# First norm of a hybrid S5 and convolution block: statistics in four batches, rows from a broadcast column, large S5 arrays loaded behind the slabs

## Chip, cores and metric

The kernel runs on one core of a Trainium2 chip. The metric is the device time of one execution in microseconds (us): the median of several. A profiled execution, taken apart from these, gives the trace.

## What is computed

One layer of a trunk over 2048 latent tokens (1024 channels) with 256 context tokens ahead of them; everything is float32. What matters here is its first sub-layer:

```python
def rmsnorm(x, g):
    y = xf * lax.rsqrt(jnp.mean(xf * xf, axis=-1, keepdims=True) + EPS)
    return y * g
...
mod_l = silu(c) @ ada_w + ada_b          # six vectors of 1024: sh1, sc1, ...
nl = rmsnorm(h_lat, norm1_g) * (1 + sc1) + sh1     # 2048 tokens
nc = rmsnorm(h_ctx, norm1_g) * (1 + csc1) + csh1   # 256 tokens
zl = nl @ w_in                           # columns: S5 input 512 | conv 2*512 | gates 2*1024
zc = nc @ w_in[:, :512]
ys_l, _ = s5_mixer(zl[:, :512], zc[:, :512], ...)  # 32 groups, both directions
yb_l = conformer_branch(zl[:, 512:1536], ...)
h_lat = h_lat + g1 * gated_merge(zl, ya_l, yb_l, w_out)
```

The second sub-layer, a gated MLP, follows and is the same in both kernels.

## The kernel before

A float32 product is made as three TensorE products (lines L462, L463, L464) of operands that are split into a high and a low part: a weight chunk `w_ch` and a block's normed tokens, `nl0` to `nl3` for the four blocks of 512 latent tokens and `nlc` for the context; `h` and `l` at a name's end are the parts. ScalarE casts the high part, VectorE or GpSimd (L453) subtracts for the low one.

`phase1` goes as follows. `ada_first` takes eight slabs of 1 MB of `ada_w` from SyncE's DMA queue, multiplies each with the two conditioning vectors (L577, two records for a product), and turns the result into columns (16 small products, L586), from which the modulation's columns come. For the norm, x is needed in two layouts: `half_stats` loads 256 tokens with the token on the partition, squares them on ScalarE (L622) with the sum in a column, and takes the root (`rstd`: GpSimd's power, then a correction on VectorE). The tokens with channels on the partition come from `xt`. `row` turns two columns into a row that stands in all partitions: a diagonal tile `dg` for each column (L630), and a product with ones (L631). For the context and block 0, `early` multiplies xt by the row (L644), and `late` scales and splits (L650 to L654) once the modulation is there; for blocks 1 to 3, `modulate` does both in one pass (L661 to L663).

Then come the "u" GEMMs, that is the S5 input: for the context 96 products of 256 columns, for each of the blocks 96 of 512, in pairs of output tiles. `u_out` copies a result out of PSUM on ScalarE (L668) and stores it from ScalarE's DMA queue (`d_u`, L671). After them come the convolution's "v" GEMMs and the gates, of 24 products each: `v_pair` has four GEMMs whose sigmoid goes to `av` on ScalarE (L840) and four that multiply it on VectorE. With every GEMM goes S5 work in the background: 32 "tables" (`tab`, one for each group: three operations on GpSimd, three on VectorE, a copy and two sines on ScalarE, L245 to L253, then a store `d_rec`), 16 iterations of `s5_ops` (products L308, L318), and 32 groups of the scan. `caw` are rows of the convolution, multiplied at L795.

The order on each engine is set by a scheduler of the framework from the program and from `urgent` regions, and each engine and each DMA queue works strictly in its order. PSUM tiles `mm` have four banks, a pair of u tiles takes two and a v GEMM one. SBUF tiles come from pools: x, xt, the S5 arenas, `tab` and `av` share eight buffers (`z8`), slabs and norm tiles six, raw weights three.

Of the kernel before, what the change touches and what calls it, by code (L numbers as in the profile page):

```python
# [9 lines left out]
F32 = mybir.dt.float32  # L10
F32R = mybir.dt.float32r
I32 = mybir.dt.int32
AF = mybir.ActivationFunctionType
# [4 lines left out]
D = 1024  # L18
# [5 lines left out]
T = 8  # L24
# [85 lines left out]
def s5_params(nc, ins, scr, st, sp, tp, ident, halfpi, psum):  # L110
# [12 lines left out]
    dma(bri, ins["s5b"])  # L123
    br, bi = bri[:, 0], bri[:, 1]
    cri = sp.big(128, 2, G, H)
    dma(cri, ins["s5c"])
    cr, ci = cri[:, 0], cri[:, 1]
    dn = sp(48, G)
    dma(dn[32:48, :], ins["s5d"])
# [93 lines left out]

    bbr, bbi = sp.big(128, G, H), sp.big(128, G, H)
# [206 lines left out]
class Net:  # L431
# [38 lines left out]
    def rstd(self, pool, ss, n, scale, out=None):  # L470

        v = self.v
        vv = pool.tile([128, n], F32, name="rs_v")
        y = pool.tile([128, n], F32, name="rs_y")
        z = pool.tile([128, n], F32, name="rs_z")
# [5 lines left out]
        out = y if out is None else out  # L481
        v.tensor_tensor(out, y, z, op=OP.mult)
        return out
# [60 lines left out]
    def consts(self):  # L544
# [7 lines left out]
        self.mhalf = cp.tile([128, 4], F32, name="mhalf")  # L552
# [44 lines left out]
    def phase1(self):  # L597
        nc, tc, ins, scr, v, a = self.nc, self.tc, self.ins, self.scr, self.v, self.a
        w_in = ins["w_in"]
        with ExitStack() as ctx:  # L600
# [12 lines left out]
            rms = small.tile([128, 18], F32, name="rms", bufs=1)  # L613

            def half_stats(i):

                x2 = self.z8("x2", [128, 2, D])
                src = ins["x"][256 * i:256 * i + 256, :] if i < 8 else ins["ctx"]
                self.dma(x2, src.rearrange("(j p) d -> p j d", p=128))
                ss = small.tile([128, 2], F32, name="nt_ss")  # L620
                for j in range(2):
                    a.activation(x2[:, j, :], x2[:, j, :], AF.Square, accum_out=ss[:, j:j + 1])  # L622
                self.rstd(small, ss, 2, 1.0 / D, rms[:, 2 * i:2 * i + 2])

            def row(i, n):

                ps = psum.tile([128, 512], F32, name="ps", tag="ax")
                for j in range(n // 128):
                    dg = small.tile([128, 128], F32, name="dg")
                    v.tensor_scalar(dg, self.ident, rms[:, 2 * i + j:2 * i + j + 1], None, op0=OP.mult)  # L630
                    self.pe.matmul(ps[:, 128 * j:128 * j + 128], self.ones, dg, start=True, stop=True)  # L631
                return ps
# [32 lines left out]
            def u_out(ps, n, m, x0s):  # L665
                ub = rp.tile([128, T, 64], F32, name="ub", tag="ub", bufs=2)
                nc_ = n // T
                a.copy(ub[:, :, :nc_], ps[:, :n].rearrange("p (c s) -> p s c", s=T)[:, ::-1, :])  # L668
                for x0 in x0s:
                    dst = scr["u"][8 * m:8 * m + 8, :, :, x0:x0 + nc_].rearrange("g h s x -> (g h) s x")  # L670
                    self.store(dst, ub[:, :, :nc_])  # L671
# [12 lines left out]
            def u_block(b):  # L684
                for ms in ((0, 1), (2, 3)):
                    pair(ms, 512, lambda k: (nl[b](0, k), nl[b](1, k)), [NCC + 64 * b])
# [3 lines left out]
            def after(k):  # L690
                if k == 0:
                    next(s5a)
                if k == 1:
                    self.dma(xc, ins["ctxt"])
                    half_stats(8)
                    early([xc[:, 4 * q:4 * q + 4] for q in range(2)], row(8, CTX)[:, :CTX], CTX)
                if k in (2, 3, 4, 5):
                    next(s5a, None)
                if k == 7:
                    for m in range(2):  # L700
                        wu[m] = self.wtile(ring, w_in, 128 * m)
                    raw_block(0)
                    for i in range(2):
                        half_stats(i)
                    early([xt[0, q] for q in range(2)], row(0, 512), 512)
# [6 lines left out]
            nl[0] = self.nl_tiles(0, "nl")  # L712
            with self.urgent():
                late(lambda k: xt[0, k // 4][:, k % 4], lambda k: nl[0](0, k), lambda k: nl[0](1, k), 0)
            for ms in ((0, 1), (2, 3)):
                pair(ms, CTX, lambda k: (nlc(0, k), nlc(1, k)), [0, NX - NCC])
            self.low = "v"
# [7 lines left out]
            for i in (2, 3):  # L725
                half_stats(i)
            prepare(1)
            for i in (4, 5, 6, 7):
                half_stats(i)
            u_block(0)  # L730
# [681 lines left out]
```

## Time and profile before

| | us |
|---|---|
| median of 3 runs | 2813.17 (2813.14 to 2813.37) |
| profiled execution | 2806.18 |
| its span, first to last instruction | 2804.4 |
| TensorE busy in the span | 2711.9 |
| VectorE, ScalarE, GpSimd busy | 1508.0, 822.7, 459.3 |

Times in the rows below are microseconds from the start of the span, in the profiled execution, which was 7.0 us shorter than the median. The granted clock of TensorE is a share of 2.4 GHz; its other level is 1.2 GHz. "L577" is line 577 of the kernel before.

### The profile page before, as it was taken

The numbers are of one execution on the slowest core, as the hardware profiler recorded it, in microseconds if no ns is written. First come the engines' busy times: TensorE is split into PE (matmuls) and PEld (weight loads), VectorE is DVE, ScalarE is ACT, GpSimd is POOL, SyncE is SP. The second block draws the span as 40 slices with busy tenths as digits, with TensorE's granted clock in tenths as the row PEclk, the third lists the DMA queues.
The fourth block names the chain that finished last, engine by engine and source line by source line (L and its number), as shares of the span: only waits on it lengthen the run. The fifth ranks groups of instructions, "written<-read, shape, count | busy, mean of one in ns | idle before, by whom it ended". The sixth has DMA issues, their size and how long they took to land.

```text
span 2804.4 us, 32119 instructions
## 1 busy us (share of the span) xinstructions
PE 2711.9 (97%) x12044; PEld 2203.2 (79%) x12044; DVE 1508.0 (54%) x2312; ACT 822.7 (29%) x1446; POOL 459.3 (16%) x504
## 2 busy tenths in 40 slices
PE   7998999999999999999999999999999989999998
PEld 3786878788887777788888888888888878787887
DVE  5867643433316788566855646556465462414154
ACT  2555412121235443243421222212222132212122
POOL 2256477667600000000000000000000000000000
PEclk8999999999999999999999999999999999999999
DMA  8645745354436576533111111111111153323143
GB/s 315 195 142 165 205 138 153 126 177 147 145 102 202 173 206 200 187 131 113 64 46 57 42 49 49 49 53 46 45 57 42 53 179 107 113 71 135 53 143 98
DMA packets 327308, 334.73 MB, mean 119 GB/s; under 512 B 95336, under 2 KB 240360, under 8 KB 324464
## 3 DMA queue, kind: packets, MB, share of 16 engines
q1 hardware_dynamic: 245680, 235.13, 27.2%
q10 hardware_dynamic: 81472, 97.54, 10.0%
q8 instruction: 95, 1.56, 0.2%
q14 instruction: 61, 0.50, 0.1%
HBM read 230.38 MB, written 102.21 MB: 119 GB/s over the span
## 4 chain that ended last, share of the span: by engine, by line
PE 75%; DVE 9%; DMA 6%; POOL 5%; issue 2%; ACT 2%; SPq 0%; ACTq 0%; POOLq 0%; DVEq 0%
PE ps L464 23%; PE ps L462 23%; PE ps L463 23%; DMA sgab<-d_sg 2%; PE ps L795 1%; DVE Hs L408 1%; PE ps L577 1%; PE ps L385 1%; POOL t L395 1%; DVE Hs L410 1%; DMA slab<-in_ada_w_dram 1%; DMA ada<-in_ada_w_dram 1%; POOL t L394 1%; POOL t L361 1%; PE ps L1112 0%
## 5 line engine op out<-in xcount | busy, mean ns | idle before, releaser
L1242 DVE SCALAR_TENSOR_TENSOR acc<-pad,fw,acc 128x1024 f32<-128x1024 f32 x352 | 450.4, 1282 | 238.9 <-ACT acc L1238 229.5
L477 POOL TENSOR_TENSOR rs_y<-rs_v,mhalf 128x1 f32<-128x1 f32 (+1 forms) x41 | 27.4, 668 | 2048.8 <-DVE rs_v L476 2048.8
L462 PE MATMUL ps<-wd,hhl 128*128 128x512 f32 x704 | 275.6, 393 | 13.5 <-ACT hhl L449 7.3
L463 PE MATMUL ps<-wd,hhl 128*128 128x512 f32 x704 | 275.7, 392 | 0.0
L464 PE MATMUL ps<-wd,hhl 128*128 128x512 f32 x704 | 275.3, 392 | 0.1
L408 DVE TENSOR_TENSOR_SCAN Hs<-m,S 64x287 f32<-64x287 f32 x64 | 68.8, 1075 | 240.5 <-POOL S L396 240.1
L453 DVE TENSOR_TENSOR hhl<-hr,hhl 128x512 fp32r<-128x512 f32 (+1 forms) x110 | 63.0, 582 | 244.4 <-ACT hhl L449 244.1
L453 DVE TENSOR_TENSOR w_ch<-w_raw,w_ch 128x512 fp32r<-128x512 f32 x134 | 106.4, 801 | 137.9 <-ACT w_ch L449 137.5
L462 PEld LDWEIGHTS ps<-wd,hhl 128*128 128x128 f32 x704 | 133.2, 189 | 43.3 <-ACT hhl L449 7.9
L449 ACT CAST w_ch<-w_raw 128x512 fp32r<-128x512 f32 x142 | 87.6, 621 | 267.2 <-PE ps L464 167.1
L463 PEld LDWEIGHTS ps<-wd,hhl 128*128 128x128 f32 x704 | 133.2, 189 | 28.6 <-DVE wd L453 1.0
L464 PEld LDWEIGHTS ps<-wd,hhl 128*128 128x128 f32 x704 | 133.1, 189 | 28.5 <-DVE hhl L453 0.8
L449 ACT CAST hhl<-hr 128x512 fp32r<-128x512 f32 (+1 forms) x110 | 57.2, 534 | 264.5 <-PE ps L464 231.3
L463 PE MATMUL ps<-nm2l,w_ch 128*128 128x512 f32 x344 | 133.8, 389 | 0.0
L464 PE MATMUL ps<-nm2h,w_ch 128*128 128x512 f32 x344 | 133.8, 389 | 0.0
L462 PE MATMUL ps<-nm0h,w_ch 128*128 128x512 f32 x344 | 133.8, 389 | 0.0
L463 PE MATMUL ps<-nm0l,w_ch 128*128 128x512 f32 x344 | 133.8, 389 | 0.0
L463 PE MATMUL ps<-nm1l,w_ch 128*128 128x512 f32 x344 | 133.8, 389 | 0.0
L463 PE MATMUL ps<-nm3l,w_ch 128*128 128x512 f32 x344 | 133.8, 389 | 0.0
L464 PE MATMUL ps<-nm0h,w_ch 128*128 128x512 f32 x344 | 133.8, 389 | 0.0
L462 PE MATMUL ps<-nm1h,w_ch 128*128 128x512 f32 x344 | 133.8, 389 | 0.0
L464 PE MATMUL ps<-nm1h,w_ch 128*128 128x512 f32 x344 | 133.8, 389 | 0.0
(370 smaller groups left out, 6354.5 us busy)
## 6 DMA issues: line engine op xcount, KB each, us to landing
w_raw<-in_ffn_w_up_dram SPq DMA_DIRECT2D x88, 256.0 KB
d_hid<-acc ACTq DMA_DIRECT2D x88, 256.0 KB
w_raw<-in_ffn_w_down_dram SPq DMA_DIRECT2D x76, 256.0 KB
grp<-d_rec SPq DMA_DIRECT2D x32, 576.0 KB
hr<-d_hid SPq DMA_DIRECT2D x66, 256.0 KB
d_sg<-sgg ACTq DMA_DIRECT2D x64, 256.0 KB
ada<-in_ada_w_dram SPq DMA_DIRECT2D x64, 256.0 KB
sgab<-d_sg SPq DMA_DIRECT2D x32, 512.0 KB
```

The source lines that it names most:

```text
L361: g_.tensor_tensor(r1, Hl, tb[:, 0:1, LAT].to_broadcast([128, 2, NCL]), op=OP.mult)
L385: nc.tensor.matmul(ps[:, :NX], sm[:, i, :], ug, start=True, stop=True)
L394: g_.tensor_tensor(t1, S, tb[:, 0:1, :].to_broadcast([128, 2, NX]), op=OP.mult)
L395: g_.tensor_tensor(t2, S[:, ::-1, :], tb[:, 1:2, :].to_broadcast([128, 2, NX]), op=OP.mult)
L408: v.tensor_tensor_scan(Hs[0:64, i, 1:1 + nsc], mb[0:64], S[0:64, i, 0:nsc], 0.0, op0=OP.mult, op1=OP.add)
L410: v.tensor_tensor_scan(Hs[64:128, i, NX - 1 - nsc:NX - 1][:, ::-1], mb[64:128], S[64:128, i, NX - nsc:NX][:, ::-1], 0.0, op0=OP.mult, op1= ...
L449: self.a.copy(hi, src)
L453: e.tensor_tensor(lo, src, hi.bitcast(F32), op=OP.subtract)
L462: mm(ps, wh, xh, start=first, stop=False)
L463: mm(ps, wh, xl, start=False, stop=False)
L464: mm(ps, wl, xh, start=False, stop=last)
L1242: v.scalar_tensor_tensor(acc[:, h], win(h, t // 3, t % 3), fw[:, i, t:t + 1], acc[:, h], op0=OP.mult, op1=OP.add)
```

## The change

The three large S5 arrays (`s5b`, `s5c`, `s5d`) are loaded where `s5_params` first needs them, at its last step, which stands behind block 0's GEMMs. The context's x and xt are loaded after slab 5, no longer after slab 1. The statistics are taken in four batches: the context; block 0; block 1; blocks 2 and 3 together. A batch has one `rstd` over 2, 4, 4 or 8 columns, one TensorE transposition of these (L626 of the kernel after), a copy to `rt`, and `row` then multiplies a column of the identity, broadcast to 128 columns, with `rt` (L639): row r of rt lands in all partitions. No diagonal tiles are left. Block 0 goes through `modulate` too. Statistics are asked a block ahead, a block's u GEMMs are two halves with the next block's `prepare` between, u_out's copy is urgent, and the program asks for 27 tables in the u phase instead of 18.

```diff
-    dma(bri, ins["s5b"])
-    dma(cri, ins["s5c"])
-    dma(dn[32:48, :], ins["s5d"])
...
+    dma(bri, ins["s5b"])
+    dma(cri, ins["s5c"])
+    dma(dn[32:48, :], ins["s5d"])
     bbr, bbi = sp.big(128, G, H), sp.big(128, G, H)
...
-            def half_stats(i):
...
-                ss = small.tile([128, 2], F32, name="nt_ss")
-                for j in range(2):
-                    a.activation(x2[:, j, :], x2[:, j, :], AF.Square, accum_out=ss[:, j:j + 1])
-                self.rstd(small, ss, 2, 1.0 / D, rms[:, 2 * i:2 * i + 2])
-
-            def row(i, n):
-
+            def stats(*halves):
+
+
+                n = 2 * len(halves)
+                ss = small.tile([128, 8], F32, name="nt_ss")[:, :n]
+                for h, i in enumerate(halves):
+                    x2 = self.z8("x2", [128, 2, D])
+                    src = ins["x"][256 * i:256 * i + 256, :] if i < 8 else ins["ctx"]
+                    self.dma(x2, src.rearrange("(j p) d -> p j d", p=128))
+                    for j in range(2):
+                        a.activation(x2[:, j, :], x2[:, j, :], AF.Square, accum_out=ss[:, 2 * h + j:2 * h + j + 1])
+                    rows_[i] = 2 * h
+                rs = self.rstd(small, ss, n, 1.0 / D)
                 ps = psum.tile([128, 512], F32, name="ps", tag="ax")
-                for j in range(n // 128):
-                    dg = small.tile([128, 128], F32, name="dg")
-                    v.tensor_scalar(dg, self.ident, rms[:, 2 * i + j:2 * i + j + 1], None, op0=OP.mult)
-                    self.pe.matmul(ps[:, 128 * j:128 * j + 128], self.ones, dg, start=True, stop=True)
+                self.pe.transpose(ps[:n, :128], rs, self.ident)
+                rt = small.tile([8, 128], F32, name="rt")
+                v.tensor_copy(rt[:n], ps[:n, :128])
+                for i in halves:
+                    rows_[i] = (rt, n, rows_[i])
+
+            def row(*halves):
+
+                ps = psum.tile([128, 512], F32, name="ps", tag="ax")
+                for h, i in enumerate(halves):
+                    rt, n, r = rows_[i]
+                    for j in range(2):
+                        o = 256 * h + 128 * j
+                        self.pe.matmul(ps[:, o:o + 128], self.ident[:n, r + j:r + j + 1].to_broadcast([n, 128]),
+                                       rt[:n], start=True, stop=True)
                 return ps
...
-                a.copy(ub[:, :, :nc_], ps[:, :n].rearrange("p (c s) -> p s c", s=T)[:, ::-1, :])
+                with self.urgent():
+                    a.copy(ub[:, :, :nc_], ps[:, :n].rearrange("p (c s) -> p s c", s=T)[:, ::-1, :])
...
-                if k == 1:
+                if k == 5:
+                    stats(8)
                     self.dma(xc, ins["ctxt"])
-                    half_stats(8)
-                    early([xc[:, 4 * q:4 * q + 4] for q in range(2)], row(8, CTX)[:, :CTX], CTX)
...
+                    stats(0, 1)
                     raw_block(0)
...
             def prepare(b):
-                raw_block(b)
-                srow[b] = row(2 * b, 512)
+
+                srow[b] = row(2 * b, 2 * b + 1)
                 with self.urgent():
                     modulate(b)
+                if b < 3:
+                    raw_block(b + 1)
+                if b < 2:
+                    stats(*((2, 3), (4, 5, 6, 7))[b])
...
+            u_ctx((0, 1))
+            prepare(0)
+            u_ctx((2, 3))
+            self.low = "v"
+            u_block(0, 0)
             prepare(1)
...
+            u_block(0, 1)
             for _ in s5a:
                 pass
...
             for b in range(1, 4):
+                u_block(b, 0)
                 if b < 3:
                     prepare(b + 1)
-                u_block(b)
-                for _ in range((0, 3, 6, 9)[b]):
+                for _ in range((0, 3, 6, 6)[b]):
+                    next(tabs, None)
+                u_block(b, 1)
+                for _ in range((0, 3, 3, 6)[b]):
                     next(tabs, None)
```

How the instructions now stand on three engines follows, first as they stood before and then as they stand after. A row is a line, an operation, out<-in and its shape; "x6" is six in a row.

SyncE's DMA queue, before, from its first load (`tp` and `sp` are the S5 arenas; xt from `ctxt` and x from `ctx` are the context):

```order
L574 DMA slab<-in_ada_w_dram 128x2048
L120 DMA tp_95<-in_s5s_dram 128x96
L123 DMA tp_95<-in_s5b_dram 128x1024
L126 DMA sp_96<-in_s5c_dram 128x1024
L129 DMA sp_97<-in_s5d_dram 16x32
L574 DMA slab<-in_ada_w_dram 128x2048
L694 DMA xt<-in_ctxt_dram 128x2048
L619 DMA x_139<-in_ctx_dram 128x2x1024
L574 DMA slab<-in_ada_w_dram 128x2048 x6
L496 DMA w_raw<-in_w_in_dram 128x4x128 x3
L638 DMA xt<-in_xt_dram 128x2048
L496 DMA w_raw<-in_w_in_dram 128x4x128
```

The same place after:

```order
L571 DMA slab<-in_ada_w_dram 128x2048
L120 DMA tp_95<-in_s5s_dram 128x96
L571 DMA slab<-in_ada_w_dram 128x2048 x5
L620 DMA x_227<-in_ctx_dram 128x2x1024
L704 DMA xt<-in_ctxt_dram 128x2048
L571 DMA slab<-in_ada_w_dram 128x2048 x2
L493 DMA w_raw<-in_w_in_dram 128x4x128 x3
L620 DMA x_316<-in_x_dram 128x2x1024
L493 DMA w_raw<-in_w_in_dram 128x4x128
L620 DMA x_320<-in_x_dram 128x2x1024
L647 DMA xt<-in_xt_dram 128x2048 x2
```

The S5 arrays went behind (they stand after block 3's xt), the context behind six slabs, and block 0's x ahead of its xt. Before, both x loads followed the second xt.

TensorE, before, from its first product to the first context GEMM (L462):

```order
L577 MATMUL ps<-slab,sc 2x512 x32
L631 MATMUL ps<-dg,ones 128x128 x3
L586 MATMUL ps<-ident,adarow 128x2 x16
L631 MATMUL ps<-dg,ones 128x128
L462 MATMUL ps<-nlch,w_ch 128x256 x3
```

The same place after:

```order
L574 MATMUL ps<-slab,sc 2x512 x24
L626 MATMUL ps<-ident,rs_y 2x128
L639 MATMUL ps<-rt,ident 128x128 x2
L574 MATMUL ps<-slab,sc 2x512 x8
L626 MATMUL ps<-ident,rs_y 4x128
L583 MATMUL ps<-ident,adarow 128x2 x16
L639 MATMUL ps<-rt,ident 128x128 x3
L462 MATMUL ps<-nlch,w_ch 128x256 x2
```

The context's transposition and rows went in among the slab products, and block 0's transposition stands ahead of the 16 products that make the modulation's columns. Further on, block 1's transposition stands after 37 of the 96 products of nl0, its rows after 48; the eight columns of blocks 2 and 3 are transposed at 0.41 of nl1.

ScalarE, before, around the first sigmoid of the v GEMMs (L840), with the tables of S5 around it (L251 to L254):

```order
L254 DMA d_rec<-tab 128x640
L840 ACT_TABLE_LOAD
L840 ACTIVATE av<-ps 128x16x32 x2
L252 ACT_TABLE_LOAD
L252 ACTIVATE tab<-tab 128x320
L840 ACT_TABLE_LOAD
L840 ACTIVATE av<-ps 128x16x32
L449 CAST w_ch<-w_raw 128x512
```

The same place after:

```order
L251 ACTIVATE tab<-tab 128x320
L254 DMA d_rec<-tab 128x640
L852 ACT_TABLE_LOAD
L852 ACTIVATE av<-ps 128x16x32 x4
L252 ACT_TABLE_LOAD
L252 ACTIVATE tab<-tab 128x320
L253 ACTIVATE tab<-tab,halfpi 128x320
```

All four sigmoids now stand together, behind the 25th table; before, the first two stood behind the 18th. The copies of block 3's first half stand behind the 9th table after the change, and the first casts of a v weight behind the 14th (before: the 12th). On TensorE every S5 operation stands three GEMMs earlier than before, while the caw products keep their place at the 11th GEMM. From the end of S5 on, the order of all engines is the same.

## Rows read from the trace of the kernel before

**Rows 1.** Windows: stretch, length; PE, PEld, DVE, ACT, POOL busy; clock, DMA, GB/s.
```profile
0.00:52.00 52.00, 35.08 (x89) 8.88 (x89) 24.75 (x128) 13.60 (x27) 9.71 (x18) 0.92 0.91 352
52.00:70.00 18.00, 16.47 (x100) 15.22 (x100) 14.56 (x24) 6.90 (x17) 6.33 (x6) 0.76 0.61 207
70.00:171.00 101.00, 94.66 (x408) 76.81 (x408) 77.64 (x155) 56.10 (x106) 41.98 (x60) 0.97 0.62 181
171.00:345.00 174.00, 162.23 (x806) 131.61 (x806) 117.56 (x229) 92.57 (x237) 92.44 (x125) 0.96 0.57 174
```

**Rows 2.** TensorE's timeline at the start: start, length, line, tile, idle before it.
```profile
6.40 8.68 PE L577 MATMUL ps<-slab,sc 128*2 128x512 f32 x16 [6.40 <-DMA slab<-in_ada_w_dram]
19.22 22.46 PE L577 MATMUL ps<-slab,sc 128*2 128x512 f32 x48 [4.15 <-DMA slab<-in_ada_w_dram]
47.93 0.80 PE L631 MATMUL ps<-dg,ones 128*128 128x128 f32 x2 [5.60 <-DVE dg L630]
48.66 1.86 PE L586 MATMUL ps<-ident,adarow 2*128 2x2 f32 x16
51.95 1.01 PE L462 MATMUL ps<-nlch,w_ch 128*128 128x256 f32 x3 [0.71 <-ACT nlch L652]
```

**Rows 3.** TensorE's longest wait from 171 to 345, and the products behind it.
```profile
PE ps L795 <- ACT tab L253: 7.3, 1, 7.3
L795 PE MATMUL ps<-caw,ctw x12: 421/421/553, 246.6 to 249.1; 128*128 128x128 f32 x12
```

**Rows 4.** Window of the longest of these waits.
```profile
233.00:256.00 23.00, 15.68 (x66) 12.93 (x65) 19.84 (x35) 10.86 (x21) 18.83 (x30) 0.78 0.40 133
```

**Rows 5.** SyncE's queue, timeline: when each load was issued.
```profile
4.78 0.44 SPq L619 DMA_DIRECT2D x<-in_ctx_dram  x1
34.09 0.37 SPq L496 DMA_DIRECT2D w_raw<-in_w_in_dram  x1
35.05 0.94 SPq L619 DMA_DIRECT2D x<-in_x_dram  x2
```

**Rows 6.** Window of the first loads; its last number is GB/s.
```profile
4.00:28.00 24.00, 17.39 (x33) 2.98 (x34) 17.22 (x106) 3.08 (x7) 0.71 (x1) 0.93 1.01 423
```

**Rows 7.** Matmuls by tile: shortest, median, longest ns, first and last start.
```profile
L462 PE MATMUL ps<-nlch,w_ch x32: 279/283/579, 52.0 to 69.2; 128*128 128x256 f32 x32
L462 PE MATMUL ps<-nl0h,w_ch x32: 388/389/628, 70.4 to 98.3; 128*128 128x512 f32 x32
L462 PE MATMUL ps<-nl3h,w_ch x32: 389/389/389, 149.3 to 170.4; 128*128 128x512 f32 x32
```

**Rows 8.** TensorE's timeline: first product of the first v GEMM.
```profile
171.92 0.50 PE L462 MATMUL ps<-nl0h,w_ch 128*128 128x512 f32 x1 [0.71 <-ACT w_ch L449]
```

**Rows 9.** VectorE from 0 to 171, by line: count, busy us, mean ns.
```profile
L630 DVE TENSOR_SCALAR dg<-ident,rms 128x128 f32<-128x128 f32 x18 | 5.6, 338 | 5.1 <-PE ps L631 4.9
```

**Rows 10.** ScalarE's timeline (ACTq: its DMA queue).
```profile
64.71 4.97 ACTq L671 DMA_DIRECT2D d_u<-ub  x3
69.72 0.62 ACT L652 CAST nl0h<-xt 128x512 fp32r<-128x512 f32 x1 [4.68 <-issue]
188.85 1.28 ACT L840 ACT_TABLE_LOAD   x1
190.14 0.60 ACT L840 ACTIVATE av<-ps 128x512 f32<-128x512 f32 x1
```

**Rows 11.** GpSimd's timeline: first operations of two groups of three tables.
```profile
151.53 1.05 POOL L245 TENSOR_SCALAR tab<-sp 128x320 f32<-128x320 f32 x2 [0.91 <-DMA d_rec<-tab]
159.28 1.05 POOL L245 TENSOR_SCALAR tab<-sp 128x320 f32<-128x320 f32 x2 [0.87 <-DMA d_rec<-tab]
```

**Rows 12.** All 32 tables: VectorE, ScalarE, GpSimd busy in one window.
```profile
85.00:345.00 260.00, 57.63 (x96) 42.87 (x96) 59.22 (x96) 0.97 0.56 168
```

**Rows 13.** TensorE's products of an S5 iteration (L308, L318), all sixteen.
```profile
171.00:345.00 174.00, 9.96 (x64) 7.65 (x64) 0.96 0.57 174
171.00:345.00 174.00, 19.24 (x128) 14.65 (x128) 0.96 0.57 174
```

More of the change, by code (lines that the diff above doesn't have):

```diff
@@ L468, in gemm, with rstd @@
             self.mm3(ps, w[k], x(k), k == 0, k == len(w) - 1)
-    def rstd(self, pool, ss, n, scale, out=None):
+    def rstd(self, pool, ss, n, scale):
         v = self.v
-        vv = pool.tile([128, n], F32, name="rs_v")
-        y = pool.tile([128, n], F32, name="rs_y")
-        z = pool.tile([128, n], F32, name="rs_z")
+        vv, y, z = (pool.tile([128, 8], F32, name=nm)[:, :n] for nm in ("rs_v", "rs_y", "rs_z"))
         v.tensor_scalar(vv, ss, scale, EPS, op0=OP.mult, op1=OP.add)
@@ L480, in rstd @@
         v.tensor_scalar(z, z, -0.5, 1.5, op0=OP.mult, op1=OP.add)
-        out = y if out is None else out
-        v.tensor_tensor(out, y, z, op=OP.mult)
-        return out
+        v.tensor_tensor(y, y, z, op=OP.mult)
+        return y
     def t16(self, name, shape=None, dt=F32R):
@@ L551, in consts @@
         v.memset(self.halfpi, PI / 2)
-        self.mhalf = cp.tile([128, 4], F32, name="mhalf")
+        self.mhalf = cp.tile([128, 8], F32, name="mhalf")
         v.memset(self.mhalf, -0.5)
@@ L612, in phase1 @@
             nl, srow, xt = {}, {}, {}
-            rms = small.tile([128, 18], F32, name="rms", bufs=1)
-            def half_stats(i):
-                x2 = self.z8("x2", [128, 2, D])
-                src = ins["x"][256 * i:256 * i + 256, :] if i < 8 else ins["ctx"]
-                self.dma(x2, src.rearrange("(j p) d -> p j d", p=128))
-                ss = small.tile([128, 2], F32, name="nt_ss")
-                for j in range(2):
-                    a.activation(x2[:, j, :], x2[:, j, :], AF.Square, accum_out=ss[:, j:j + 1])
-                self.rstd(small, ss, 2, 1.0 / D, rms[:, 2 * i:2 * i + 2])
@@ L625, in row @@
-            def row(i, n):
-                ps = psum.tile([128, 512], F32, name="ps", tag="ax")
-                for j in range(n // 128):
-                    dg = small.tile([128, 128], F32, name="dg")
-                    v.tensor_scalar(dg, self.ident, rms[:, 2 * i + j:2 * i + j + 1], None, op0=OP.mult)
-                    self.pe.matmul(ps[:, 128 * j:128 * j + 128], self.ones, dg, start=True, stop=True)
+            rows_ = {}
+            def stats(*halves):
[9 more added lines that the diff above has]
+                rs = self.rstd(small, ss, n, 1.0 / D)
+                ps = psum.tile([128, 512], F32, name="ps", tag="ax")
+                self.pe.transpose(ps[:n, :128], rs, self.ident)
[3 more added lines that the diff above has]
+                    rows_[i] = (rt, n, rows_[i])
@@ L682, in pair, with u_block @@
                     u_out(ps, n, m, x0s)
-            def u_block(b):
-                for ms in ((0, 1), (2, 3)):
-                    pair(ms, 512, lambda k: (nl[b](0, k), nl[b](1, k)), [NCC + 64 * b])
+            def u_block(b, h):
+                pair((2 * h, 2 * h + 1), 512, lambda k: (nl[b](0, k), nl[b](1, k)), [NCC + 64 * b])
             xc = self.z8("xt", [128, 8, CTX])
@@ L692, in after @@
                     next(s5a)
-                if k == 1:
+                if k == 5:
+                    stats(8)
                     self.dma(xc, ins["ctxt"])
-                    half_stats(8)
-                    early([xc[:, 4 * q:4 * q + 4] for q in range(2)], row(8, CTX)[:, :CTX], CTX)
-                if k in (2, 3, 4, 5):
+                if k in (2, 3, 4, 6):
                     next(s5a, None)
                 if k == 7:
+                    early([xc[:, 4 * q:4 * q + 4] for q in range(2)], row(8)[:, :CTX], CTX)
                     for m in range(2):
                         wu[m] = self.wtile(ring, w_in, 128 * m)
+                    stats(0, 1)
                     raw_block(0)
-                    for i in range(2):
-                        half_stats(i)
-                    early([xt[0, q] for q in range(2)], row(0, 512), 512)
             self.ada_first(psum, after)
@@ L711, in phase1, with u_ctx @@
                 wu[m] = self.wtile(ring, w_in, 128 * m)
[L712 to L715, printed above, removed]
+            def u_ctx(ms):
                 pair(ms, CTX, lambda k: (nlc(0, k), nlc(1, k)), [0, NX - NCC])
-            self.low = "v"
             def prepare(b):
-                raw_block(b)
-                srow[b] = row(2 * b, 512)
+                srow[b] = row(2 * b, 2 * b + 1)
                 with self.urgent():
                     modulate(b)
-            for i in (2, 3):
-                half_stats(i)
+                if b < 3:
[7 more added lines that the diff above has]
+            u_block(0, 0)
             prepare(1)
-            for i in (4, 5, 6, 7):
-                half_stats(i)
-            u_block(0)
+            u_block(0, 1)
             for _ in s5a:
```

## Prediction

> **What bounds the kernel now.** I read the windows by stage first, then TensorE's timeline and its waits, and then the queues that stand behind each wait. In the windows [rows 1] the reader sees TensorE busy for 35.1 of the first 52 us, 16.5 of the next 18 (at a granted clock of 0.76), 94.7 of the 101 us of the u GEMMs and 162.2 of the 174 us after them. So TensorE is the bound, and a change ahead of 345 us can win only idle or slow time: 17 + 1.5 + 6.3 + 11.8 us of idle at the most. The timeline of the start [rows 2] tells where the 17 us are: 6.40 us until the first slab, 4.15 until the third, 5.60 until the first diagonal tile of block 0, 0.71 until the first context tile. The context GEMMs start at 51.95.
>
> After the u GEMMs the waits are of another kind: the longest, 7.3 us, has the convolution's caw products wait behind a table's sine on ScalarE until 246.6 [rows 3]. It comes from the S5 work in the background, of which VectorE and GpSimd are nearly full (19.8 and 18.8 of the 23 us around that wait) [rows 4].
>
> **The change, part by part, as times in the profiled span.**
>
> *Slabs.* By 4.78 SyncE had issued s5b, s5c and the context's xt and x (the last at 4.78 [rows 5]), 0.5 + 0.5 + 1 + 1 MB by the shapes in the order, all of it ahead of the third slab. At 423 GB/s [rows 6] that is 7.4 us of transfer. It now stands behind all slabs or behind six of them. The first 16 product records [rows 2] are those of two slabs, so the wait of 4.15 us is for the third; it lands 7 us sooner and the wait goes whole. The last slab doesn't take its place: eight slabs and the context's 2 MB are 10.5 MB, 25 us from about 4, and the 64 records end at 41.7 - 4.15 = 37.5.
>
> *Rows of block 0.* The 5.60 us were spent on x's squares, a chain of small VectorE operations and two diagonals; x came late because its loads (35.05) stood behind a weight load that waits for a buffer (34.09) and behind xt [rows 5]. Now the first x load stands ahead of that weight load and xt behind both. The 4-column transposition is, however, in TensorE's order ahead of the 16 small adarow products, so it is a new wait of the same place: x's second load still goes behind the 34.09 load, lands near 37.5, is squared by 39.5, and three microseconds of small operations and the copy put the products at about 42.5 instead of 48.66. From there to the first context GEMM it was 51.95 - 48.66 = 3.3 us [rows 2], which stays. First context GEMM: **45.8**, 6.2 earlier. Bounds: nothing of the 5.60 is won (47.8), or all (42.2).
>
> *Context GEMMs.* They took 52.0 to 69.2 [rows 7] at clock 0.76, and nl0 started at 70.4. VectorE, 14.6 busy of these 18 us, loses the block's early and late passes and diagonals of 338 ns [rows 9] there. I take 2 us of the 18 (between 0 and 3): nl0 starts at **62**, 8.3 earlier.
>
> *New operations on TensorE and VectorE.* The 18 diagonal products become 18 row products of the same 128 columns, and 4 transpositions come in. The trace shows neither form; the nearest row is two diagonal products in 0.80 us [rows 2], so 4 x 0.4 = 1.6 us at that price, nothing at the least. I put 2.4 us on the four blocks with the waits of these against the GEMMs around them. VectorE loses 18 diagonals (5.6 us [rows 9]) and gains four small copies; it isn't the bound there, and I cost it at nothing.
>
> *u GEMMs.* A block that waits for nothing takes 21.8 us (its first and last L462 start at 149.3 and 170.4 [rows 7], 93 products apart; 96 of them), four take 87.2; they took 101. The idle is from casts that stand behind ScalarE's own d_u issues: three issues at 64.71 hold it 4.97 us and the cast of nl0h idles 4.68 [rows 10]. Halved blocks and earlier rows take part of that away. Against it, block 1's statistics are asked before block 0's GEMMs, and ScalarE still squares in order behind such issues, so the transposition, in TensorE's order after 37 of the block's 96 products, can come late: I leave 6 us of waits (0 to 12). The u phase then ends at 62 + 87.2 + 2.4 + 6 = **158**, 13 earlier than before (170.4 and three products more).
>
> *The wait that takes their place.* The ScalarE order is what decides here. Before, the first two sigmoids of the v GEMMs stood behind 18 tables; now all four stand behind 25, and the first casts of v's weights behind 14 (before: 12). The fifth v GEMM needs the PSUM bank of the first, which its sigmoid frees. By the order 9 tables are out when block 3's first half ends, near 147. Sixteen remain. A table with nothing between costs (159.28 - 151.53) / 3 = 2.58 us [rows 11]; its own work is 57.6 / 32 = 1.80 us on VectorE and 59.2 / 32 = 1.85 on GpSimd [rows 12], which makes 1.85 the least and 3.65 the most, if the two never overlap. Stretches with evictions between them were slower than 2.58, so I take 2.75: 147 + 44 = 191, and a table load of 1.28 and a sigmoid of 0.6 [rows 10] make 193. The GEMMs before it end at 158 + 21.8 = 180 (four v GEMMs are 96 products, like a block). So TensorE waits about **13 us** in all, at the first v GEMM (casts) and at the fifth, which starts at 193. Before, it started at 171.9 [rows 8] + 21.8 = 193.7: at this point the whole gain has been given back.
>
> *What is left of it.* The seven tables are work done ahead. S5's iterations stand three GEMMs earlier in TensorE's order: eight instead of four ahead of the caw products. An iteration's products are 9.96 / 16 + 19.24 / 16 = 1.8 us [rows 13]. So from 193, with 7 GEMMs (38 us) and 8 iterations (14.6), these products come at 246, where before they came at 246.6 [rows 3] with four iterations fewer done, which are 4 x 1.8 = 7.3 us of products: 0.6 + 7.3 = 8 us ahead. What becomes of smaller waits behind it I count as nothing, and nothing for the clock either: a new wait of 13 us will cool it as the one of 7.3 did (0.78 in those 23 us [rows 4]).
>
> **Sum.** 8 us off the profiled execution's 2806.2, whose span is 2804.4, gives 2798. That execution lies 7.0 under the median of 2813.2, and I keep that distance: **2805 us**. 0.2% is 5.6 us, about what a measurement of this kernel tells from no change.
>
> **Rivals.**
>
> 1. *Tables are quicker, and the wait is short.* For it: 2.58 is measured, VectorE has fewer norm passes beside them, and 1.85 is the floor. At 2.3 us a table the fifth GEMM starts at 147 + 36.8 + 1.9 = 186, the new wait is 6, and 7 us more of the gain stay: 2798. Against it: it was never seen so quick. Chance 0.15.
>
> 2. *Nothing is left.* Where VectorE can't feed eight S5 iterations in the 53 us after 193 (it was busy 19.8 of 23 us beside GEMM 11 [rows 4]), TensorE waits for S5 instead, up to the 8 us: 2813. The same result comes if the u phase keeps the bounds against it: 2 us for no faster rows and 6 more of late statistics, with the tables as much later; and also if the change doesn't do what it says, the slabs not being earlier since something else than the loads ahead holds them: 4.2 us lost, half of the gain. Chance 0.20.
>
> 3. *Slower, by the tables.* This is one mechanism at one place: sixteen tables between block 3 and the sigmoids, on VectorE and GpSimd, which may hold each other up. At 3.65 us each the fifth GEMM starts at 147 + 58.4 + 1.9 = 207, 14.4 later than I forecast: 2805 + 14.4 = 2819, and a microsecond or two more where S5 waits for the same engines: **2820**. It decides from 2.75 + 8 / 16 = 3.25 us a table (no gain), and a measurable loss comes from 3.6. For it: GpSimd's idle in this stretch is mostly for VectorE; against it: three tables in 7.75 us [rows 11], where 3 x 3.65 would be 10.95. Chance 0.15.
> The Trainium skill, "SBUF — State Buffer", section "Who interferes with whom", states that a VectorE instruction with two SBUF inputs and a GpSimd instruction that reads SBUF lock each other out for the whole instruction. By that rule the tables would cost the full 3.65 and this rival would be the likeliest. The 7.75 us disagree: 3.2 of the 10.95 us did overlap.
>
> **Chances.** My forecast, a gain of 4 to 13 us (2800 to 2809), has 0.50. Of it some 0.07 lies within 0.2%. Faster: 0.43 + 0.15 = 0.58. Same: 0.07 + 0.20 = 0.27. Slower 0.15. The range leaves out half of rival 1 at the low end and two thirds of rival 3 at the high end: 2795 to 2819; the likeliest case's own is 2800 to 2809.
>
> **What would show it.** After the change: no wait between slab products and their end near 37.5; first nlch GEMM near 45.8; first nl0 GEMM near 62; u phase ending near 158; then waits of TensorE for w_ch and for the sigmoid, together about 13 us, and the fifth v GEMM near 193; the caw products near 246 with little wait. The forecast is wrong if the tables run at another rate than 2.5 to 3.2 us, if block statistics hold the u GEMMs by more than 12 us, or if S5 on VectorE becomes the bound between 193 and 345.

## The result, and the profile after

The changed kernel is slower: 2840.56 us (2832.19 to 2842.97, 4 runs) against 2813.27 us of the kernel before, a ratio of 1.0087 (95% interval 1.0062 to 1.0111). The profiled execution took 2842.97 us, its span 2841.1, mean granted clock 0.978. The two traces lie 36.7 us apart and the medians 27.3, as the trace of the kernel before lay 7.0 under its median.

The windows of the changed kernel, at the places of [rows 1]:

```profile
0.00:52.00 52.00, 40.36 (x118) 14.94 (x118) 30.64 (x135) 17.04 (x35) 13.46 (x21) 0.90 0.91 356
52.00:70.00 18.00, 17.68 (x109) 15.62 (x109) 12.30 (x18) 7.93 (x15) 2.28 (x2) 1.00 0.87 289
70.00:171.00 101.00, 88.77 (x359) 71.58 (x360) 62.14 (x108) 51.30 (x97) 29.97 (x46) 0.86 0.50 155
171.00:345.00 174.00, 146.14 (x705) 117.24 (x704) 117.69 (x226) 78.31 (x222) 98.71 (x132) 0.91 0.53 167
```

Up to 70 us TensorE does more than before, 58.0 us of 70 (before 51.6). From 70 to 171 it is busy for 88.8 us and the granted clock is 0.86 (94.7 at 0.97), and from 171 to 345 for 146.1 us at 0.91 (162.2 at 0.96). The loss is made there, behind the start. Counted at the granted clock, TensorE has done some 29 us less work by 345 than before; 15.5 us of that is more idle time and the rest the lower clock (an estimate from these windows and [rows 1]).

TensorE's timeline at the start, against [rows 2]:

```profile
6.52 22.91 PE L574 MATMUL ps<-slab,sc 128*2 128x512 f32 x48 [6.52 <-DMA slab<-in_ada_w_dram]
30.64 7.03 PE L574 MATMUL ps<-slab,sc 128*2 128x512 f32 x16
41.98 0.37 PE L626 MATMUL ps<-ident,rs_y 128*4 128x128 f32 x1 [4.31 <-DVE rs_y L479]
42.29 1.86 PE L583 MATMUL ps<-ident,adarow 2*128 2x2 f32 x16
45.59 0.80 PE L462 MATMUL ps<-nlch,w_ch 128*128 128x256 f32 x2
```

The wait for the third slab is gone and the slab products end at 37.7. The new wait of 4.31 us for block 0's statistics stands ahead of the 16 small products, and the first context GEMM starts at 45.6.

Matmuls by tile, with the first and last start of each L462, against [rows 7]:

```profile
L462 PE MATMUL ps<-nlch,w_ch x32: 279/283/582, 45.6 to 60.8; 128*128 128x256 f32 x32
L462 PE MATMUL ps<-nl0h,w_ch x32: 387/389/795, 61.1 to 100.1; 128*128 128x512 f32 x32
L462 PE MATMUL ps<-nl1h,w_ch x32: 389/389/795, 100.8 to 128.8; 128*128 128x512 f32 x32
L462 PE MATMUL ps<-nl2h,w_ch x32: 389/389/499, 129.5 to 151.9; 128*128 128x512 f32 x32
L462 PE MATMUL ps<-nl3h,w_ch x32: 389/389/389, 152.5 to 173.6; 128*128 128x512 f32 x32
```

nl0 starts 9.3 us sooner than before (61.1), nl1 already 1.8 us later (100.8 against 99.0 in the trace before), nl3 3.2 us later (152.5 against 149.3). Block 0 alone takes 39.7 us, and nothing is left of the start's gain.

Where block 0 loses it is seen on ScalarE. Its timeline from 60 to 77:

```profile
60.96 0.54 ACTq L681 DMA_DIRECT2D d_u<-ub  x1
62.51 1.04 ACT L622 ACTIVATE x<-x 128x1024 f32<-128x1024 f32 x1
74.37 0.37 ACT L678 COPY ub<-ps 128x256 f32<-128x256 f32 x1 [10.11 <-DMA d_u<-ub]
76.72 1.04 ACT L622 ACTIVATE x<-x 128x1024 f32<-128x1024 f32 x1
```

A copy of the context's results (`ub`, L678) waits 10.1 us for the store of an earlier copy, which was issued at 60.96, as there are two buffers. Behind it, in ScalarE's order, stand three of block 1's four squares (L622). So block 1's statistics end late, and TensorE's transposition, which stands among block 0's products, has this row in the timeline:

```profile
80.06 0.37 PE L626 MATMUL ps<-ident,rs_y 128*4 128x128 f32 x1 [10.37 <-DVE rs_y L479]
```

The wait has a second price, in the windows of 4 us behind it, where the first number after the busy times is the granted clock:

```profile
82.00:86.00 4.00, 4.00 (x12) 2.86 (x11) 0.00 (x0) 0.59 (x1) 0.00 (x0) 0.50 1.09 390
90.00:94.00 4.00, 4.00 (x13) 3.09 (x13) 4.00 (x7) 3.13 (x6) 0.00 (x0) 0.65 0.29 66
94.00:98.00 4.00, 4.00 (x19) 3.31 (x18) 4.00 (x7) 2.69 (x5) 0.00 (x0) 1.00 0.56 181
```

From 80 to some 93 TensorE is busy without a gap, yet at 0.50, its lower level of 1.2 GHz; then at 1.00.

Then the tables. ScalarE's timeline, the sines of the 9th and the 25th table and what stands behind them:

```profile
162.84 0.55 ACT L253 ACTIVATE tab<-tab,halfpi 128x320 f32<-128x320 f32 x1
214.32 0.55 ACT L253 ACTIVATE tab<-tab,halfpi 128x320 f32<-128x320 f32 x1
216.28 1.28 ACT L852 ACT_TABLE_LOAD   x1 [1.06 <-DMA d_rec<-tab]
217.58 2.06 ACT L852 ACTIVATE av<-ps 128x512 f32<-128x512 f32 x4
```

And the fifth v GEMM, in TensorE's timeline:

```profile
218.23 0.79 PE L462 MATMUL ps<-nl0h,w_ch 128*128 128x512 f32 x1 [16.82 <-ACT av L852]
```

It waits 16.8 us for the sigmoid and starts at 218.2. In the trace of the kernel before it started at 193.9 without a wait:

```profile
193.91 0.39 PE L462 MATMUL ps<-nl0h,w_ch 128*128 128x512 f32 x1
```

Sixteen tables took 214.9 - 163.4 = 51.5 us, 3.2 us each. GpSimd's timeline shows what stood between them:

```profile
165.73 1.04 POOL L245 TENSOR_SCALAR tab<-sp 128x320 f32<-128x320 f32 x2 [0.56 <-ACT tab L253]
173.53 1.05 POOL L245 TENSOR_SCALAR tab<-sp 128x320 f32<-128x320 f32 x2 [0.92 <-DMA d_rec<-tab]
176.80 0.93 POOL L291 TENSOR_TENSOR ca<-sp,sp 128x288 f32<-128x288 f32 x1
190.43 1.72 POOL L245 TENSOR_SCALAR tab<-sp 128x320 f32<-128x320 f32 x2
```

The three tables that begin at 165.7, with nothing between, take 7.8 us. Those that begin at 173.5 take 16.9: operations of the first S5 iterations (L291 and others) go between them, on GpSimd and on VectorE.

What TensorE waits for from 171 to 345, against [rows 3]:

```profile
PE ps L462 <- ACT av L852: 16.8, 1, 16.8
PE ps L464 <- DVE w_ch L453: 5.2, 2, 3.2
PE ps L308 <- DVE ab L281: 4.7, 1, 4.7
```

And the caw products behind it:

```profile
L807 PE MATMUL ps<-caw,ctw x72: 272/275/275, 284.0 to 342.5; 128*128 128x128 f32 x72
```

They start at 284.0 and not at 246.6; seven S5 iterations are done by then, four before. The windows from the fifth v GEMM to the caw products, first in the kernel before and then in the changed one:

```profile
193.90:246.60 52.70, 45.38 (x218) 36.67 (x216) 36.47 (x61) 26.60 (x65) 33.33 (x49) 0.95 0.38 129
218.20:284.00 65.80, 57.40 (x249) 44.38 (x250) 45.76 (x83) 31.79 (x97) 37.89 (x50) 0.89 0.45 146
```

TensorE's idle time there is nearly the same, 7.3 and 8.4 us; the clock is lower.

### The profile page after: what moved, and what is told of

It reads as the page before. It is cut to its first block, busy times and chain, and to the rows that moved or that the text cites. A ratio compares the mean times of both kernels' runs of the same rounds, so it can differ in the third digit from the quotient of the medians.

```text
span 2841.1 us, 32087 instructions
## 1 busy us (share of the span) xinstructions
PE 2723.5 (96%) x12048; PEld 2210.9 (78%) x12048; DVE 1495.1 (53%) x2273; ACT 812.8 (29%) x1438; POOL 452.9 (16%) x497
## 4 chain that ended last, share of the span: by engine, by line
PE 71%; DVE 9%; DMA 7%; POOL 6%; issue 4%; ACT 2%; SPq 0%; ACTq 0%; POOLq 0%; DVEq 0%
PE ps L464 23%; PE ps L462 23%; PE ps L463 22%; DMA sgab<-d_sg 2%; DVE Hs L408 1%; PE ps L807 1%; POOL t L395 1%; DMA w_raw<-in_w_in_dram 1%; DVE Hs L410 1%; DMA ada<-in_ada_w_dram 1%; POOL t L394 1%; PE ps L385 1%; POOL t L361 1%; POOL tab L245 0%; POOL S L396 0%
## 5 line engine op out<-in xcount | busy, mean ns | idle before, releaser
L475 POOL TENSOR_TENSOR rs_y<-rs_v,mhalf 128x1 f32<-128x1 f32 (+3 forms) x36 | 23.2, 645 | 2082.6 <-DVE rs_v L474 2082.6
L462 PE MATMUL ps<-wd,hhl 128*128 128x512 f32 x704 | 275.1, 392 | 13.0 <-ACT hhl L449 7.8
L462 PEld LDWEIGHTS ps<-wd,hhl 128*128 128x128 f32 x704 | 132.8, 189 | 42.7 <-ACT hhl L449 8.2
L462 PE MATMUL ps<-nm0h,w_ch 128*128 128x512 f32 x344 | 133.8, 389 | 0.0
L462 PE MATMUL ps<-nm1h,w_ch 128*128 128x512 f32 x344 | 133.8, 389 | 0.0
L462 PE MATMUL ps<-nm2h,w_ch 128*128 128x512 f32 x344 | 133.8, 389 | 0.0
L464 PE MATMUL ps<-nm2h,w_ch 128*128 128x512 f32 x344 | 133.8, 389 | 0.0
L462 PE MATMUL ps<-nm3h,w_ch 128*128 128x512 f32 x344 | 133.8, 389 | 0.0
```

What stands on the lines that cost most here:

```text
L462: mm(ps, wh, xh, start=first, stop=False)
L464: mm(ps, wl, xh, start=False, stop=last)
```

## The experiments

After the result I had two theories. **A**: the loss is made where the four sigmoids stand behind 25 tables. **B**: it is made in the u phase, whose late statistics make everything later, the tables too. Kernels of one group ran on the same chip; the ratio is to the kernel before, run beside them.

| kernel | median us (runs) | before us | ratio, 95% interval |
|---|---|---|---|
| change | 2840.6 (4) | 2813.3 | 1.0087, 1.0062 to 1.0111 |
| tab18 | 2820.0 (7) | 2813.2 | 1.0024, 1.0013 to 1.0036 |
| nourg | 2836.0 (4) | 2813.2 | 1.0077, 1.0055 to 1.0100 |
| ub3 | 2835.1 (4) | 2813.2 | 1.0074, 1.0053 to 1.0094 |
| tab18_ub3 | 2808.2 (10) | 2813.2 | 0.9984, 0.9973 to 0.9995 |
| before_tab27 | 2841.9 (4) | 2814.0 | 1.0095, 1.0080 to 1.0110 |
| before_s5late | 2810.3 (10) | 2814.0 | 0.9983, 0.9973 to 0.9993 |
| tab18_ub3_split | 2811.6 (10) | 2814.0 | 0.9987, 0.9977 to 0.9997 |
| tab21_ub3 | 2816.4 (10) | 2814.0 | 1.0016, 1.0005 to 1.0026 |
| fill | 2810.1 (11) | 2814.5 | 0.9983, 0.9974 to 0.9992 |
| tab15_ub3 | 2821.5 (12) | 2814.5 | 1.0025, 1.0014 to 1.0036 |
| before_s5ctx | 2810.2 (11) | 2814.5 | 0.9985, 0.9976 to 0.9993 |
| tab15_split | 2819.7 (11) | 2814.5 | 1.0016, 1.0007 to 1.0024 |

**tab18: the tables paced as before.**

```diff
-                for _ in range((0, 3, 6, 6)[b]):
-                    next(tabs, None)
                 u_block(b, 1)
-                for _ in range((0, 3, 3, 6)[b]):
+                for _ in range((0, 3, 6, 9)[b]):
```

> The changed kernel with the tables of the u phase paced as before (18 asked for, 3, 6 and 9 behind blocks 1 to 3); the sigmoids then stand behind 16 tables, not 25, everything else is the change. Theory A (the loss is made where the sigmoids stand behind 25 tables): the 16.8 us wait for av falls under 5, the fifth v GEMM starts before 205 (218.2 in the change), and the time is 24 us or so less than the change, 2812 to 2822. Theory B (the loss is made in the u phase, whose statistics come late and make the tables late): u phase and first tables stay late, later waits of S5 take the place of this one, 2832 to 2842.

It is 20.5 us faster than the change. The fifth v GEMM in its timeline of TensorE:

```profile
196.60 0.80 PE L462 MATMUL ps<-nl0h,w_ch 128*128 128x512 f32 x1 [5.34 <-ACT av L850]
```

It starts 21.6 us sooner than in the change, though the transposition still waits 10.4 us in block 0. The wait for av is 5.3 us, a little over the 5 that I expected. Theory A holds about three quarters of the loss.

**nourg and ub3: what holds block 1's squares.** In nourg `u_out`'s copy is no longer urgent; in ub3 it has a third buffer.

```diff
-                with self.urgent():
-                    a.copy(ub[:, :, :nc_], ...)
+                a.copy(ub[:, :, :nc_], ...)        # nourg
...
-                rt = small.tile([8, 128], F32, name="rt")
+                rt = small.tile([8, 128], F32, name="rt", bufs=1)         # ub3
-                ub = rp.tile([128, T, 64], F32, name="ub", tag="ub", bufs=2)
+                ub = rp.tile([128, T, 64], F32, name="ub", tag="ub", bufs=3)
```

> The changed kernel without the urgent region on u_out's copy: block 1's squares go ahead of the context's third and fourth copies on ScalarE. Theory A: the transposition's wait of 10.4 us goes, but 25 tables still stand ahead of the sigmoids and are done little sooner, so the time is 2834 to 2842. Theory B: the wait goes, nl1 starts near 90 (100.8 in the change), and 10 to 12 us of it reach the end: 2826 to 2832.

> The changed kernel with three buffers for u_out's copies instead of two (and one for the row tile rt, to make room): the copy that held ScalarE 10.1 us for its buffer's store no longer waits for that store. Theory A: 2834 to 2842. Theory B: as without the urgent region, the transposition waits under 3 us, nl1 starts near 90, 2826 to 2832. If the squares wait for something else than that copy (their own loads), the wait stays over 7 us and both are wrong on this point.

The wait in block 0 goes in both: nl1 starts at 89.4 in nourg and 84.5 in ub3, 11 and 16 us sooner. Of that 4.5 and 5.5 us come to the end, which isn't clear of noise: the intervals of both overlap that of the change. In block 1 the transposition of the eight columns now waits (7.2 us in nourg, 5.1 in ub3). TensorE's waits of ub3 from 0 to 171, and its fifth v GEMM:

```profile
PE ps L626 <- DVE rs_y L479: 9.5, 3, 5.1
```

```profile
208.09 0.79 PE L462 MATMUL ps<-nl0h,w_ch 128*128 128x512 f32 x1 [16.88 <-ACT av L852]
```

In ub3 the u phase ends 11 us sooner than in the change, the fifth v GEMM starts 10 sooner, and it still waits 16.9 us for the sigmoid. In nourg that wait is only 3.0 us, but the third v GEMM has already waited 8.0 us, for block 3's own copies, which are no longer urgent and stand among the tables on ScalarE:

```profile
192.01 0.79 PE L462 MATMUL ps<-nl2h,w_ch 128*128 128x512 f32 x1 [7.99 <-ACT ub L677]
```

Its fifth v GEMM starts at 207.5, as late as in ub3. The times are those of theory A: what the u phase wins is lost again at the tables, whichever operation stands behind them. That the held copy is what makes block 1's statistics late, as B had it, is shown as well.

**tab18_ub3: both edits.**

> Both edits: 18 tables asked for in the u phase and three buffers for the copies. If A and B each hold a part, the sum of both: 24 and 10 us less than the change, 2800 to 2810, under the kernel before. A alone: 2812 to 2822 as with the tables alone. B alone: 2826 to 2832.

2808.2 us, faster than the kernel before by a ratio of 0.9984 (0.9973 to 0.9995) and 11.9 us faster than tab18. With few tables ahead the third buffer is worth 11.9 us, against 5.5, not clear of noise, in the change. So both theories hold a part, A the larger.

**before_tab27: the pace alone, in the kernel before.**

```diff
-                for _ in range((0, 3, 6, 9)[b]):
+                for _ in range((0, 6, 9, 12)[b]):
```

> The kernel before with 27 tables asked for in its u phase (6, 9 and 12 behind blocks 1 to 3) instead of 18: the change's table pace alone, so that all four sigmoids stand behind 25 tables. Theory A (the pace makes the loss by itself): a wait of 12 to 20 us for av, the fifth v GEMM starts at 208 to 216 (193.9 before), and the time is 2825 to 2835. Rival (the pace costs only since the change's u phase lets the tables start late): the wait is under 8 us and the seven tables done ahead pay for it, 2808 to 2818.

This one edit loses as much as the whole change, more than theory A had said. The fifth v GEMM in TensorE's timeline, and the caw products:

```profile
210.33 0.80 PE L462 MATMUL ps<-nl0h,w_ch 128*128 128x512 f32 x1 [11.76 <-ACT av L840]
```

```profile
L795 PE MATMUL ps<-caw,ctw x84: 272/275/275, 276.0 to 344.9; 128*128 128x128 f32 x84
```

The u phase ended 2 us later than before, no more; the fifth GEMM waits 11.8 us and starts 16.4 us late, and by the caw products it has become 29.4 us, with seven S5 iterations done instead of four, three more, which are 5.5 us of products. The wait for tables that stood ahead of the caw products (7.3 us) is gone, as it is in the change, and waits for S5's operands (6.6 us) and for casts (3.2) have come instead. The rival, that the tables done ahead pay for the wait, is out: they don't pay.

**before_s5late and before_s5ctx: the loads alone, in the kernel before.** The first moves the three S5 loads as the change does; the second also takes the context's loads and statistics at slab 5.

```diff
-                if k == 1:
+                if k == 5:                                # before_s5ctx
                     self.dma(xc, ins["ctxt"])
                     half_stats(8)
...
```

> The kernel before with the loads of s5b, s5c and s5d alone moved to the last step of the S5 parameters. 1 MB less stands ahead of the third slab, 2.4 us of its wait of 4.15. Theory: 1.5 to 3 us at the first context GEMM (49 to 50.5, was 52.0), which the context's own loads still hold back, and nothing that can be measured at the end: 2808 to 2815. Rival: the S5 arrays are late for S5 now and the tables with them, 2816 to 2825.

> The kernel before with its loads as in the change, and nothing else: the S5 arrays at the last step of the parameters, the context's loads and statistics after slab 5. Theory: the wait for the third slab (4.15 us) goes whole, the first context GEMM starts at 47.5 to 48.5 (48.7 with the S5 arrays alone), the rest as with these alone: 2807 to 2812. Rival: the context's statistics, late now, hold the transposed rows and the context GEMMs, which start no sooner than 48.7 or later.

Both are faster than before by about 4 us (0.9983 and 0.9985), more than I held to be measurable. The first context GEMM starts at 48.7 and 48.8, 3.3 us sooner, and the 3.3 us are still there at the first caw products (243.3 and 243.2). That the context's loads move too adds nothing: the wait for the third slab goes, and the one for block 0's diagonals grows from 5.6 to 8.0 us. On that point the rival came nearer.

**tab18_ub3_split: blocks 2 and 3 in two batches.**

```diff
-                if b < 2:
-                    stats(*((2, 3), (4, 5, 6, 7))[b])
+                if b < 3:
+                    stats(2 * b + 2, 2 * b + 3)
```

> The best kernel so far (18 tables, three copy buffers) with the statistics of blocks 2 and 3 in two batches, each asked a block ahead, instead of one batch of eight columns. Theory: the wait of 5.0 us for the eight-column transposition in block 1 and the stretch of lower clock behind it go; block 1's GEMMs take 22 to 25 us (32.7), and at least half of the 8 to 10 us reaches the end: 2798 to 2804. Rival: the transposition moves ahead in TensorE's order as well and waits as long, or the gain goes into the wait for tables before the caw products (8.9 us there): 2805 to 2811.

The u phase ends 2.3 us sooner than with one batch (160.4 against 162.7), not 8; block 1 takes 29.6 us, not 22 to 25; the total is not better (0.9987 against 0.9984). The wait in block 1 is 3.9 us instead of 5.0, as the transposition moved ahead in TensorE's order as well, from 39 to 21 products into the block. The rival was right.

**tab21_ub3, tab15_ub3 and tab15_split: other counts.** The ranges are (0, 3, 6, 12) and (0, 3, 6, 6); the sigmoids stand behind 19 and 13 tables.

> 18 tables and three copy buffers, but 21 tables asked for (3, 6 and 12), so that the sigmoids stand behind 19 tables. Theory A: each table more ahead of the sigmoids costs its 2.6 to 3 us on the wait for av (3.8 to some 12 us) and gives it back at the caw products' wait for tables only in part: 2810 to 2818. Rival: the wait of 8.9 us at the caw products falls by as much as the other grows: 2805 to 2810.

> Three copy buffers, and 15 tables asked for (3, 6, 6): the sigmoids stand behind 13 tables. Theory (each table ahead of the sigmoids costs only while the fifth v GEMM waits for av, 3.8 us with 18): that wait goes, and the tables that are later show at the caw products, whose wait grows from 8.9 to 12 to 16 us: 2806 to 2814, no better than 18. Rival: fewer is better on this side too, 2799 to 2805.

> 15 tables asked for, three copy buffers, and the statistics of blocks 2 and 3 in two batches. The u phase ended at 160 with two batches and the caw products came late (255.5) only because of the order. Theory: its sum is 2803 to 2809. Rival: as with 18 tables and two batches, 2809 to 2814.

Three tables more than 18 cost 0.0032 in the ratios, 9 us, and the wait for av is 11.3 us, as theory A had it. Three fewer cost 0.0041, 11 to 12 us: the expectation missed, since it looked at the caw products alone. With 15, a weight cast of the thirteenth GEMM stands behind a run of tables on ScalarE; its timeline, and TensorE's:

```profile
249.58 0.55 ACT L253 ACTIVATE tab<-tab,halfpi 128x320 f32<-128x320 f32 x1
250.52 0.62 ACT L449 CAST w_ch<-w_raw 128x512 fp32r<-128x512 f32 x1
```

```profile
251.19 0.79 PE L462 MATMUL ps<-nl0h,w_ch 128*128 128x512 f32 x1 [11.05 <-ACT w_ch L449]
```

So the same wait stands at another place, 11 us for a cast. The two batches don't help there either (2819.7, above both ranges that I had given).

**fill: TensorE kept at work through the wait.** In tab18_ub3, six products of x's squares that nothing uses stand ahead of the eight-column transposition.

```diff
+                if n == 8:
+                    for _ in range(6):
+                        self.pe.matmul(ps, self.ones, x2[:, 0, :512], start=True, stop=True)
                 self.pe.transpose(ps[:n, :128], rs, self.ident)
```

> 18 tables and three copy buffers, with six idle products of 512 columns (12 records of some 0.43 us, 5 us) put ahead of the eight-column transposition; they read the squares of the last x tile, so they start when these are there, and nothing uses them. TensorE then works through most of the wait of 5.0 us. Theory (the wait's price is mostly the lower granted clock behind it, 0.75 over 99 to 118): the clock stays at 1.0 there, block 1's GEMMs take 27 to 29 us instead of 32.7, the u phase ends 4 to 6 us sooner (158 to 159; 162.7), 2802 to 2809. Rival (the clock has another cause than that wait): it stays under 0.8 and the u phase ends no sooner, 2807 to 2812.

The windows of tab18_ub3, first, and of fill:

```profile
99.00:118.00 19.00, 18.97 (x68) 15.05 (x69) 13.48 (x22) 10.59 (x20) 0.84 (x2) 0.75 0.43 115
```

```profile
91.00:99.00 8.00, 5.34 (x12) 2.20 (x12) 5.04 (x12) 3.65 (x8) 5.49 (x8) 1.00 0.98 315
99.00:118.00 19.00, 18.87 (x87) 15.37 (x87) 13.64 (x23) 11.69 (x21) 1.02 (x3) 1.00 0.46 133
```

The clock stays at 1.00 where it was 0.75. The time doesn't follow: with the products the transposition moved from 39 to 24 products into the block, where 3.0 us of wait and 5.4 us of filling replace 5.0 us of wait. Block 1 takes 32.0 us instead of 32.7, so the clock gave back some 4 us, and the longer stop took them. On the clock the theory was right; on the block's time and on the end of the u phase (162.0) it missed, and the total shows no gain (0.9983 against 0.9984).

## Why the prediction was wrong

The start was right, step by step. "The 64 records end at ... 37.5": 37.7. "First context GEMM: 45.8": 45.6. "nl0 starts at 62": 61.1. The new transpositions and rows, at 2.4 us for four blocks, were too cheap: block 2, which waits for nothing, takes 23.0 us and block 3, without rows, 22.0, so they are 1 us a block at full clock and double at the lower one.

The *u GEMMs* step named the right mechanism, squares behind ScalarE's queue and a transposition in TensorE's order, and mis-sized it: "I leave 6 us of waits (0 to 12)". The waits were 10.4 and 2.2 us, and the lower clock behind them had no place in my sum: block 0's 39.7 us are 21.8 + 10.4 and 7.5 us of clock and rows. The phase ended at 174.5, not at 158. I also thought of the d_u issues; it was a copy that waited for its buffer's store. Nor were casts the main wait of this phase before, as the step says: TensorE waited 2.9 and 2.1 us there for rows' diagonals, and 0.7 for a cast.

Two steps failed behind it, and they make the loss. *The wait that takes their place* had the place right and the size not: it put the fifth v GEMM at 193, level with before, and it came at 218.2, 24 us later than before. The ninth table was done at 163 instead of "near 147", mostly as the u phase was late (152.4 in ub3, where it ended 11 us sooner). A table took 3.2 us and not 2.75, since S5 operations went in between; the order showed that, and I took the rate of three tables with nothing between. Also, before the change the first two sigmoids stand behind 16 finished tables, not the 18 that are given ahead of the prediction. By its own rule the fifth GEMM is then at 163.4 + 51.5 + 1.9 = 217; it was 218.2.

The other is *What is left of it*: "The seven tables are work done ahead ... 8 us ahead". It let 7 GEMMs and 8 iterations follow the fifth GEMM's start with no wait and at full clock: "What becomes of smaller waits behind it I count as nothing, and nothing for the clock either". The wait of 7.3 us for tables did go, but 8.4 us of waits for S5's own operands and casts took its place, and a lower clock (0.89, before 0.95). So 7 GEMMs and 7 iterations, some 51 us of work, took 65.8. TensorE is the bound and its work is the same in any order, so a lead of S5 wins only what it takes from TensorE's waits and lower clock, and these grew. At the caw products the change is 37.4 us later than before with 5.5 us more of products done: 32 behind, where my sum had it 8 ahead. Of these 40 us the fifth GEMM's start makes 25 and the stretch behind it 15. before_tab27 shows the two steps wrong without the other edits: with the u phase only 2 us late, the same pace loses 28 us.

Two of the prediction's own signs of being wrong came up, both narrowly: statistics held the u GEMMs by more than 12 us (12.6), and the tables ran at 3.2 us.

Rival 3 was this place, with 3.65 us a table: 2820. Its price was about as far from the 3.2 measured as mine. Its sum was still 20 us short: the fifth GEMM came 11 us later than its 207, and behind that it kept the lead of 8 us. The Trainium skill's rule that stood with it ("SBUF — State Buffer", "Who interferes with whom") isn't needed for the 3.2 us: three tables without S5 operations took 173.5 - 165.7 = 7.8 us in the changed kernel too, as in [rows 11]. These 7.8 us speak against the rule less than the prediction says, for its 10.95 adds up durations of operations that had stretched beside each other. Two rows of one form from VectorE's timeline before, the first beside GpSimd's L249, the second alone:

```profile
155.54 0.73 DVE L247 SCALAR_TENSOR_TENSOR tab<-sp,tab 128x320 f32<-128x320 f32 x1
157.26 0.54 DVE L248 SCALAR_TENSOR_TENSOR tab<-sp,tab 128x320 f32<-128x320 f32 x1
```

Alone, a table's six operations take by that trace 1.57 us on VectorE and 1.44 on GpSimd, 9.0 for three tables, so the overlap that is sure is 1.3 us and not 3.2.

Put together by the runs: the pace costs 20 us in the change, 27 with the third buffer and 28 in the kernel before; the held copy 5 to 12; the S5 arrays behind the slabs gain 4. One line moves both the tables and S5's iterations, and no run parted them, say by 27 tables with the sigmoids put ahead of them on ScalarE: what the wait for the sigmoid costs by itself stays open. What the batches and the broadcast rows gain by themselves wasn't run alone; with pace and copy mended, the whole stands at 0.9984, and the move of the S5 arrays alone at 0.9983. So no gain of theirs can be measured here.

## What to carry to other kernels

Where one engine is the bound, price an edit by the waits and the lower clock that it takes from or gives to that engine, up to the end of the stretch that it reorders, and not by how far ahead some background work comes. Before work is moved ahead, look at what stands behind it on each in-order engine: here a sigmoid that frees a PSUM bank, a cast of weights, squares behind a copy. When a change bundles a pace with a cure, run the pace alone in the old kernel: one line here carried the whole loss.

## What the runs showed of the hardware

A wait of TensorE can cost more than its length. After the 10.4 us wait the granted clock stood at 0.50 for some 13 us although TensorE was busy throughout, and after a wait of 5.0 us it was 0.75 over 19 us; with idle products in the wait, which left 3.0 us of it, it stayed at 1.00. The Trainium skill ("TensorE: Matmul & The Clock Gate", "HAM oscillation — how this bites in real kernels") says that TensorE, when it waits long enough for its data, falls to the lower clock and begins its next work there; these rows agree, and fill shows it by an edit. A short wait can go either way: after one of 2.9 us in the kernel before (until 80.3) the clock was 0.62 from 80 to 84, while the 3.0 us that were left in fill did nothing to it.

A small store can be late behind large loads: the store issued at 60.96 freed its buffer at 74.37, while the DMA engines moved 280 GB/s (61 to 80), most of it SyncE's loads. That the loads held it wasn't tried.
